# The FFN in four groups of tokens in place of three

## The chip, the cores and the metric

One core of a Trainium2 chip runs the kernel. The metric is the device time of one execution in microseconds, lower is better. Five engines matter: TensorE (PE; its weight loads are listed apart as PEld), VectorE (DVE), ScalarE (ACT), GpSimd (POOL) and SyncE (SP), which issues nearly all DMAs from one queue, in order.

## What is computed

One layer of a hybrid network, over a prompt (16 meta tokens and 2,048 frames) and a sample of 64 frames: 2,128 tokens of width 1,024. Every large product is taken in two float32r parts, as three matmuls (hi by hi, hi by lo, lo by hi).

```python
hn = rms_norm(x, norm_mix_g);  proj = hn @ w_in
o_att = diff_attention(...)      # 4 heads, causal by blocks for the prompt
o_lru = rg_lru(conv(lx)) * gelu(lg)
o_gla = gla_blocked(gq, gk, gv, log_g) * silu(gog)
x = x + concat([o_att, o_lru, o_gla]) @ w_out
hn = rms_norm(x, norm_ffn_g)
u = hn @ ffn_w_up                               # 1024 -> 2816
uc = causal_dwconv(u, ffn_conv_w, ffn_conv_b)   # 3 taps along the tokens
x = x + (gelu(uc) * (hn @ ffn_w_gate)) @ ffn_w_down
y = rms_norm(x, norm_final_g)
```

## The kernel before

The work falls into four kinds. **The projection** (`win`) multiplies six blocks of tokens by W_in. **The mixers** are two streams: `attention`, 36 units (9 chunks of tokens by 4 heads; each prompt chunk is 256 tokens and sees all keys before it), and `recurrent`, 9 chunks of RG-LRU and GLA. Their outputs go to a DRAM tensor, OT. **The FFN** takes the tokens in groups (`FGROUPS`, L67), one pass over all FFN weights per group (`ffn_group`, L1478).

A pass loads the group's rows of OT into `h2h` and `h2l` (one buffer each per block) and its residual x into `x2`. Then `wout` (L1372) multiplies by W_out, eight column tiles of 24 matmuls per block, adds to x2 (L1429) and sums the squares. `norm_ffn` turns the sums into a factor on all partitions (L383, L407, L412, L418, L393) and writes the normed rows over `h2h` and `h2l` (`normed`, L425). Then for each of 22 feature tiles `up_gate` makes two products of 24 matmuls per block (L1288), with the convolution and the gelu between, and `down` (L1337) adds finished feature tiles to x2 (L1361): two tiles at a time in all passes but the last, four in the last. After the last `down`, `final` scales x2 by its norm (L1466, L1468) and stores y. A group's x2 buffers come free only when they have been stored.

Per block, W_out has 192 matmuls, up and gate 1,056 and down 528: 1,776, whatever the block's width. With three groups the blocks are 512; 512; and 336, 256 and 512 tokens.

Each weight comes as 128x1024 parts (512 KB), one queue of parts for the whole kernel in order of use, two raw buffers and three split ones (`w_load`, `w_split`): ACT rounds the hi part, POOL (two of three) or DVE makes the lo part.

The order of the instructions is made in two steps. `Flow` merges the streams by their estimated progress: the next step comes from the stream that is least advanced for its given whole time. It decides the order of emission, which is also an instruction's priority number; the attention's numbers are lowered by 30,000 and the recurrent stream's by 16,000, the norms' by 50,000. A list scheduler then gives each engine, at each moment of its own estimate, the ready instruction with the lowest number.

```python
        for g in range(NFG - 1):
            for c, ts in enumerate(CHUNKS):
                if TILES[ts[0]][0] < FOFF[g + 1]:
                    while not (att_done[c] and rec_done[c]):
                        yield None
            yield from ffn_group(g)
    flow.run((dense(), 1875e3, 0), (attention(), 560e3, 30000), (recurrent(), 616e3, 16000))
    mstack.close()
    open3()
    flow.run((ffn_group(NFG - 1), 1.0, 0))
```

`dense` is the projection and all passes but the last. While they run, products of dense kind have three PSUM banks (`ps_w`). The last pass is emitted behind the mixers' memory: its rows, x2 and gated tiles lie where the mixers' were (`open3`), it has five more banks, and its loads are paced two at a time. With several blocks, the order of W_out's column tiles lets one block's norm be made while the other blocks' last tiles are multiplied.

Of the kernel before, what the change touches and what calls it, by code (L numbers as in the profile page):

```python
# [24 lines left out]
FFN = 2816  # L25
# [17 lines left out]
# token tiles: the sample's frames and the meta tokens, then the prompt's frames by 128  # L43
# [7 lines left out]
# the FFN's features as they are summed at a time  # L51
# [5 lines left out]
def due(g, ff):  # L57
    """the features' runs that are summed after the products of tile ff"""
    lag = 1 if g == NFG - 1 else 2
    return [q for q, r in enumerate(quads(g)[:-1]) if r[-1] + lag == ff]  # L60


# the blocks of tiles that the input projection takes, in two slots: each goes once round the projection's units, from
# the unit where it joins
WBLOCKS = [[0, 1, 2], [3, 4, 5], [6, 7, 8], [9, 10, 11], [12, 13, 14], [15, 16]]
# the groups of tokens that the FFN takes per pass over its weights, by blocks
FGROUPS = [[512], [512], [336, 256, 512]]  # L67
# the k-tiles that ACT and Pool scale at the end, by block
SHARE = [[1, 3, 5, 7], [1, 4, 7], [1, 3, 5, 7]]
NFG = len(FGROUPS)  # L70
FOFF = [sum(map(sum, FGROUPS[:g])) for g in range(NFG)]
# what the mixers take at a time: the sample with the meta tokens, then pairs of tiles
# [15 lines left out]
NPAR1 = PAR["bdm"][0]  # the rest is the mixers'  # L88
# [21 lines left out]
class Flow:  # L110
    """Order of emission: streams (generators of estimated times) merged so that they advance together."""
# [4 lines left out]
    def run(self, *streams):  # L116
        """streams: (generator, its whole time, how far it goes before the others); None from one: it waits"""
# [21 lines left out]
def tile_hymba_step(ctx, tc, xT, xkT, cache_v, wi, wo, wu, wg, wd, par, sgla, c_msk, yT_p, yT_s, nkT_p, nv_p, lh_p, lc_p, gs_p, fc_p,  # L139
# [74 lines left out]
    # ------------------------------------------------------------------ weights: one queue of parts, split ahead of use  # L214
# [58 lines left out]
    # ------------------------------------------------------------------ set-up  # L273
# [47 lines left out]
    def log1p_exp(out, tmp, z, n):  # L321
        """out = log1p(exp(-|z|)), by artanh's series in (1-t)/(3+t), t = tanh(|z|/2)."""
# [21 lines left out]
    # ------------------------------------------------------------------ norm and transposition, hi and lo  # L344
    def boost(gen, off):
        """the steps of gen, ahead of others by priority; a step after (cost, 0): in its place"""
# [12 lines left out]
    def idle(steps):  # L359
        """other products come between"""  # L360
        for _ in range(steps):
            yield 100

    def add_square(acc, k, x, small, pool=False):
        """acc += x^2, over the k-tiles"""
# [9 lines left out]
    def rsqrt_rows(acc, n, small, rb, direct=False):  # L375
        """acc: the squares of n tokens, summed up to partitions; then the tokens' norm, on all partitions"""
# [19 lines left out]
    def runs(cuts):  # L396
        """the cuts of 128 tokens together, and the shorter one"""
        full = [j for j, (_, w) in enumerate(cuts) if w == P]
        out = [(P, full[0], full[-1] + 1)] if full else []
        return out + [(w, j, j + 1) for j, (_, w) in enumerate(cuts) if w < P]  # L400
# [8 lines left out]
    def spread(r, dg, cuts, bank, tag):  # L409
        """r's rows as columns, on all partitions"""  # L410
# [10 lines left out]
    def normed(rb, gain, xs, small, H, pool=True):  # L421
        """H's hi and lo of xs by gain and norm"""
# [12 lines left out]
    def h_tiles(widths, pool, tags=("hh", "hl")):  # L435
        """hi and lo per block: [128, 8, n]"""
# [3 lines left out]
    # ------------------------------------------------------------------ W_in  # L440
    p1 = ExitStack()
    # (where the first slot and the rows lie, the outputs are loaded first after them)
# [32 lines left out]
    def first_rows(H):  # L475
        """the first block's rows go in without their norm, which is put to the products"""
# [25 lines left out]
    def columns(out, blk, ps):  # L502
        """products of the block's tokens as columns"""
# [5 lines left out]
    def rows(out, t, ps):  # L509
        """products of a tile's tokens as rows"""  # L510
        nc.scalar.activation(out=out, in_=ps, func=AF.Copy, scale=row_scale.get(t, 1.0))

    def pieces(blk):
        """(columns of the block, sample or prompt, position there)"""
# [80 lines left out]
    def win():  # L595
        H, norms = {}, {}
        for s_ in range(WSTEPS):
            u = s_ % len(UNITS)
            kind = UNITS[u][0]
            for i, blk in enumerate(WBLOCKS):  # L600
                # the block's norm is ahead of the step that it joins by as many steps as the slot is free
# [50 lines left out]
    # ------------------------------------------------------------------ the sample's cached keys  # L652
    def cached_keys():
        for h in range(4):
            ck = mp.tile([P, PAST], F32, tag="K", name="ck", bufs=2)
            if h < 2:
                # not before the first products
# [8 lines left out]
    # ------------------------------------------------------------------ mixers' outputs  # L666
    def put_ot(o, src, kt, tok0, n, scale=None):
        """scale src: [128, n] float32, tokens tok0.. of k-tile kt of the mixers' output; o: [128, 2, >= n]"""
# [8 lines left out]
    # ------------------------------------------------------------------ RG-LRU, feature-major  # L677
# [93 lines left out]
    # ------------------------------------------------------------------ GLA: blocks of 128 tokens, the decays within  # L771
    # a block by halving (every exponent is at most 0)
    def gla(c):
# [45 lines left out]
        # from and to the blocks' ends  # L819
# [30 lines left out]
        # attention within the blocks, transposed: [j, head, i]  # L850
# [40 lines left out]
        # outputs [i, (head, e)], their norm per head, and the states  # L891
# [62 lines left out]
    # ------------------------------------------------------------------ differential attention: (chunk of queries, head)  # L954
    def plan(nblk):
        """the keys' chunks of at most 512: the blocks of 128, and the meta tokens' 16 more"""
# [9 lines left out]
    class Unit:  # L966
# [26 lines left out]
        def p(self, ci, ti, m):  # L993
            """the exponentials of a chunk, a tile of queries, a map: [128, ..]"""
# [6 lines left out]
    # in halves: a map's  # L1001
    slots = {"free": 2 * NPC}

    def unit_S(u):
        """scores, chunk-wise exponentials and their statistics"""
# [618 lines left out]
```

## Time and profile before

| | us |
|---|---|
| three runs | 2980.53, 2981.39, 2983.62 (median 2981.39) |
| span of the profiled execution | 2982.7 |

The page gives no time of the profiled execution other than its span, which is 1.3 us over the median of the runs. A row of the trace gives an instruction's start, its duration, its line and what it writes from what. Matmuls overlap in the pipeline (a 512-column matmul is shown as 390 to 400 ns long), so what matmuls cost is read from their spacing: so many in so many microseconds. In a table by stretches, each engine has its busy time and, in brackets, its number of instructions; then come TensorE's granted clock (1.00 is full speed, 2.4 GHz), the DMA engines' busy share and GB/s.

### The profile page before, as it was taken

Reading aid. Unit: us, or ns where it says so; the run is one execution under the profiler, and the core shown is the slowest. Engines: PE = TensorE matmul, PEld = TensorE weight load, DVE = VectorE, ACT = ScalarE, POOL = GpSimd, SP = SyncE. Lnnn points to the kernel's source line nnn. Section 1 sums busy time; section 2 is a strip of 40 time slices with the busy share of each in tenths; the row PEclk is TensorE's granted clock in tenths of the full one; section 3 lists DMA queues with packets and bytes.
Section 4 is the critical chain, followed back from the end, with each engine's and each line's share of the span. In section 5 each row is a group of like instructions: output and inputs, shape, how many; then the busy total and the mean of one; then the engine's idle time right before and its main releaser. Section 6 shows DMA issues by size and latency. Waiting matters only on the chain. (4 is left out here: it accounts for less than half of the span.)

```text
span 2982.7 us, 44483 instructions
## 1 busy us (share of the span) xinstructions
PE 2846.8 (95%) x16031; PEld 2505.3 (84%) x16031; DVE 2087.4 (70%) x3829; ACT 1276.4 (43%) x2737; POOL 1135.1 (38%) x1310
## 2 busy tenths in 40 slices
PE   7999999999899998998998999999999999999998
PEld 7988899988777887877776787878889999989997
DVE  7677685878889899899989877545565444444445
ACT  5354554555555464564454443333242222223233
POOL 4435534434435545355335444333232222212122
PEclk9999999999999999999999999999999999999999
DMA  7675664755763444443563343463111111111111
GB/s 241 200 216 145 183 212 149 206 182 165 239 195 117 127 148 124 122 151 120 190 199 113 123 146 98 130 212 128 43 36 44 44 48 43 43 43 43 43 43 69
DMA packets 235307, 382.23 MB, mean 128 GB/s; under 512 B 26278, under 2 KB 165294, under 8 KB 235086
## 3 DMA queue, kind: packets, MB, share of 16 engines
q1 hardware_dynamic: 234942, 379.38, 40.8%
q8 instruction: 127, 2.08, 0.3%
q14 instruction: 94, 0.77, 0.1%
q10 hardware_dynamic: 144, 0.01, 0.0%
HBM read 305.15 MB, written 74.16 MB: 127 GB/s over the span
## 5 line engine op out<-in xcount | busy, mean ns | idle before, releaser
L253 POOL TENSOR_TENSOR wlo<-raw,whi 128x1024 fp32r<-128x1024 f32 (+1 forms) x202 | 491.2, 2433 | 790.1 <-ACT whi L154 725.6
L154 ACT ACTIVATE whi<-raw 128x1024 fp32r<-128x1024 f32 (+2 forms) x308 | 322.5, 1047 | 542.3 <-PE pd L1355 265.0
L1355 PE MATMUL pd<-gh,whi 128*128 128x512 f32 (+2 forms) x880 | 317.1, 364 | 23.8 <-DVE x L1361 19.1
L1052 ACT ACTIVATE pc<-ps_sc,NB 128x512 f32<-128x512 f32 (+6 forms) x400 | 224.2, 561 | 260.7 <-DVE NB L1051 213.0
L1288 PE MATMUL pu<-h2l,whi 128*128 128x512 f32 (+2 forms) x880 | 315.5, 359 | 4.6 <-DVE h2l L160 4.2
L1288 PE MATMUL pu<-h2h,whi 128*128 128x512 f32 (+2 forms) x880 | 316.3, 359 | 2.3 <-ACT h2h L154 2.2
L1288 PE MATMUL pg<-h2h,wlo 128*128 128x512 f32 (+2 forms) x880 | 314.5, 357 | 2.2 <-POOL wlo L253 1.7
L1288 PE MATMUL pg<-h2h,whi 128*128 128x512 f32 (+2 forms) x880 | 316.2, 359 | 0.3 <-DVE cc L1323 0.3
L1355 PE MATMUL pd<-gl,whi 128*128 128x512 f32 (+2 forms) x880 | 315.8, 360 | 0.3 <-DVE gl L160 0.3
L1355 PE MATMUL pd<-gh,wlo 128*128 128x512 f32 (+2 forms) x880 | 315.1, 358 | 0.0
L1288 PE MATMUL pg<-h2l,whi 128*128 128x512 f32 (+2 forms) x880 | 314.9, 358 | 0.0
L1288 PE MATMUL pu<-h2h,wlo 128*128 128x512 f32 (+2 forms) x880 | 314.7, 358 | 0.0
L1361 DVE TENSOR_TENSOR x<-x,pd 128x512 f32<-128x512 f32 (+2 forms) x320 | 193.9, 614 | 160.8 <-PE pd L1355 159.0
L1312 DVE SCALAR_TENSOR_TENSOR cc<-uh,prm,cc 128x512 f32<-128x512 f32 (+4 forms) x264 | 190.7, 729 | 162.0 <-ACT cc L1310 158.6
L631 PE MATMUL ps_w<-hh,whi 128*128 128x384 f32 (+2 forms) x768 | 259.2, 340 | 15.3 <-ACT whi L154 10.6
L1051 DVE TENSOR_REDUCE NB<-ps_sc 128x1 f32<-128x512 f32 (+6 forms) x400 | 208.7, 528 | 75.1 <-PE ps_sc L1049 74.0
L631 PE MATMUL ps_w<-hl,whi 128*128 128x384 f32 (+2 forms) x768 | 259.7, 339 | 0.5 <-DVE hl L160 0.5
L631 PE MATMUL ps_w<-hh,wlo 128*128 128x384 f32 (+2 forms) x768 | 256.4, 336 | 0.3 <-DVE wlo L160 0.3
L1355 PEld LDWEIGHTS pd<-gh,whi 128*128 128x128 f32 x880 | 166.7, 190 | 50.8 <-DVE x L1361 24.9
L157 POOL TENSOR_SCALAR pc<-pc,fr 128x512 f32<-128x512 f32 (+4 forms) x200 | 158.7, 811 | 92.3 <-DVE fr L1072 68.7
L1288 PEld LDWEIGHTS pu<-h2l,whi 128*128 128x128 f32 x880 | 165.9, 189 | 26.8 <-DVE h2l L160 5.7
L1288 PEld LDWEIGHTS pu<-h2h,whi 128*128 128x128 f32 x880 | 166.3, 189 | 24.7 <-ACT h2h L154 3.2
(330 smaller groups left out, 7090.4 us busy)
## 6 DMA issues: line engine op xcount, KB each, us to landing
raw<-in_wi SPq DMA_DIRECT2D x74, 512.0 KB
raw<-in_wu SPq DMA_DIRECT2D x66, 512.0 KB
raw<-in_wg SPq DMA_DIRECT2D x66, 512.0 KB
raw<-in_wd SPq DMA_DIRECT2D x66, 512.0 KB
Kc<-KHL SPq DMA_DIRECT2D x48, 512.0 KB
V<-VHL SPq DMA_DIRECT2D x48, 512.0 KB
Q<-QHL SPq DMA_DIRECT2D x64, 256.0 KB
raw<-in_wo SPq DMA_DIRECT2D x24, 512.0 KB
```

Source lines behind the costliest of these rows:

```text
L154: nc.scalar.activation(out=out, in_=in_, func=AF.Copy, scale=scale)
L157: nc.gpsimd.tensor_scalar(out, in_, s, 1.0, ALU.mult, ALU.mult)
L253: nc.gpsimd.tensor_tensor(out=lo[:, :n], in0=t[:, :n], in1=f(hi[:, :n]), op=ALU.subtract)
L631: nc.tensor.matmul(ps[:, :n], lhsT=wx, rhs=hx, start=st_, stop=sp_)
L1051: nc.vector.tensor_reduce(NB[:qw, ti, m, ci:ci + 1], ps[:qw, :kt_], AX.X, ALU.min)
L1052: nc.scalar.activation(out=pv_[m][:qw, :kt_], in_=ps[:qw, :kt_], func=AF.Exp, scale=-1.0, bias=NB[:qw, ti, m, ci:ci + 1], accum_out=SS[:qw ...
L1288: nc.tensor.matmul(ps[:, :n], lhsT=w_[wi_][:, k * P:(k + 1) * P], rhs=hx, start=(k == 0 and i3 == 0), stop=(k == KT - 1 and i3 == 2))
L1312: nc.vector.scalar_tensor_tensor(out=cc[:, :m], in0=uh[:, w:w + m], scalar=cw[w], in1=cc[:, :m], op0=ALU.mult, op1=ALU.add)
L1355: nc.tensor.matmul(ps[:, :n], lhsT=w_, rhs=g_[:, o:o + n], start=(j == 0 and i3 == 0), stop=(j == len(gts) - 1 and i3 == 2))
L1361: nc.vector.tensor_tensor(x2[b, ct], x2[b, ct], ps[:, :n], ALU.add)
```

## The change

The last group loses its block of 512 tokens, and this block becomes a group of its own, which `dense` takes as its third pass. The blocks' widths stay 512, 512, 512, 336, 256. The estimated whole times that `Flow` is given are 2,409 in place of 1,875 for `dense`, and 700 in place of 616 for the recurrent stream; the attention's 560 stays. The rest adapts to two blocks in the last group: what is loaded, the order of blocks in its last `down`, and which tiles ACT and POOL scale at the end (block 0: three, block 1: four; before, block 0: four, block 1: three, block 2: four). Comments went too; they are left out here.

```diff
-FGROUPS = [[512], [512], [336, 256, 512]]
-SHARE = [[1, 3, 5, 7], [1, 4, 7], [1, 3, 5, 7]]
+FGROUPS = [[512], [512], [512], [336, 256]]
+SHARE = [[1, 4, 7], [1, 3, 5, 7]]
...
         if done:
-            bs = (2, 0, 1) if nb == 3 else range(nb)
+            bs = range(nb)
...
         if len(blocks) > 1:
             load_out(1)
-            load_out(2)
             load_x2(0, [0, 1])
-            load_x2(1, [2])
         else:
             load_x2(-1, [0])
...
-                if k in SHARE[b if g == NFG - 1 else 1]:
+                if k in SHARE[b if g == NFG - 1 else 0]:
...
-    flow.run((dense(), 1875e3, 0), (attention(), 560e3, 30000),
-             (recurrent(), 616e3, 16000))
+    print("FLOW",flow.run((dense(), 2409e3, 0), (attention(), 560e3, 30000),
+             (recurrent(), 700e3, 16000)))
```

## Rows read from the trace of the kernel before

**Rows 1.** The page: the span, the engines' busy time over it, and two lines of the span in 40 slices (tenths busy).
```profile
span 2982.7 us, 44483 instructions
PE 2846.8 (95%) x16031; PEld 2505.3 (84%) x16031; DVE 2087.4 (70%) x3829; ACT 1276.4 (43%) x2737; POOL 1135.1 (38%) x1310
PE   7999999999899998998998999999999999999998
DVE  7677685878889899899989877545565444444445
```

**Rows 2.** The table by stretches: the projection; the first pass; the second pass beside mixers and after them; the last pass's step from W_out to up; the rest of it; the end. Columns: stretch and its length, then PE, PEld, DVE, ACT, POOL busy, granted clock, DMA share, GB/s.
```profile
0.00:800.00 800.00, 750.44 (x4880) 709.42 (x4880) 594.47 (x1265) 409.15 (x1006) 352.20 (x398) 0.97 0.63 192
800.00:1480.00 680.00, 641.18 (x3146) 523.51 (x3147) 606.40 (x1178) 354.73 (x820) 319.02 (x390) 0.97 0.48 148
1480.00:1925.00 445.00, 421.91 (x2091) 345.87 (x2091) 354.33 (x578) 211.31 (x436) 194.02 (x191) 0.98 0.42 131
1925.00:2048.00 123.00, 120.27 (x529) 99.53 (x528) 71.06 (x87) 39.55 (x52) 47.08 (x47) 0.99 0.57 186
...
2148.00:2176.00 28.00, 21.48 (x121) 18.11 (x121) 27.03 (x46) 13.59 (x30) 14.32 (x17) 0.96 0.09 33
2176.00:2964.00 788.00, 787.50 (x4660) 715.61 (x4659) 378.07 (x588) 218.07 (x349) 178.26 (x241) 1.00 0.13 42
2964.00:2983.00 19.00, 4.05 (x17) 2.76 (x15) 10.94 (x22) 5.34 (x11) 9.96 (x11) 0.63 0.58 210
```

**Rows 3.** Where mixers and passes stand. First the last step of an attention unit (L1182, one per unit), counted on DVE in two stretches, and its 28th and last occurrence; then a late step of a recurrent chunk (L907, four per chunk) with its first and last start; then the last `down` matmul of the second pass.
```profile
0.00:1344.00 1344.00, 12.40 (x28) 0.97 0.57 174
1344.00:1930.00 586.00, 3.77 (x8) 0.98 0.43 136
L1182 DVE SCALAR_TENSOR_TENSOR oSs<-oSs,g,ps_on x1: 461/461/461, 1342.6 to 1342.6; 128x256 f32<-128x256 f32 x1
L1182 DVE SCALAR_TENSOR_TENSOR oSs<-oSs,g,ps_on x1: 476/476/476, 1922.9 to 1922.9; 128x256 f32<-128x256 f32 x1
L907 PE MATMUL ps_r<-gvr,qkd x36: 376/379/601, 148.1 to 1725.8; 128*128 128x256 f32 x32, 64*128 64x256 f32 x4
2051.70 0.40 PE L1355 MATMUL pd<-gl,whi 128*128 128x512 f32 x1
```

**Rows 4.** Spacing of matmuls. First up and gate (L1288), then down (L1355), in 54.5 us of the second pass after the mixers; then three pieces of the chain that ended last, in the last pass: 24 matmuls of 512, of 336 and of 256 columns (start, length, count).
```profile
1971.70:2026.20 54.50, 43.68 (x192) 36.00 (x192) 1.00 0.40 126
1971.70:2026.20 54.50, 11.35 (x49) 9.07 (x49) 1.00 0.40 126
2272.30 5.60 PE pu L1288 x24
2283.50 3.72 PE pu L1288 x24
2293.75 2.83 PE pg L1288 x24
```

**Rows 5.** The step from one pass to the next, in order of time (start, duration, engine, line, what). Ahead of the first pass: the first load of rows and the first W_out matmul. From the first pass to the second: the loads of x2 and the first addition to it. From the second pass to the last: the first scaling of x2, the stores of y, the next loads of x2.
```profile
807.40 0.36 SPq L148 DMA_DIRECT2D h2h<-OT  x1
816.22 0.40 PE L1423 MATMUL pd<-h2h,whi 128*128 128x512 f32 x1
1510.86 2.00 SPq L148 DMA_DIRECT2D x<-in_xT  x3
1520.57 1.27 DVE L1429 TENSOR_TENSOR x<-x,pd 128x512 f32<-128x512 f32 x2
2064.47 0.75 DVE L1468 SCALAR_TENSOR_TENSOR x<-x,prm,ps_nb 128x512 f32<-128x512 f32 x1 [0.79 <-PE ps_nb L418]
2065.24 5.47 SPq L151 DMA_DIRECT2D out_y_prompt<-x  x7
2070.88 0.94 SPq L148 DMA_DIRECT2D x<-in_xT  x2
```

**Rows 6.** The second pass's step from W_out to up, in order of time: the last W_out matmul, the last sum of squares, the factor, the first normed rows, the first up matmul.
```profile
1562.58 0.39 PE L1423 MATMUL pd<-h2l,whi 128*128 128x512 f32 x1
1565.21 2.43 DVE L370 TENSOR_TENSOR acc<-acc,sq 128x512 f32<-128x512 f32 x1
1574.40 0.60 ACT L393 ACTIVATE acc<-ps_nb 128x512 f32<-128x512 f32 x1 [0.97 <-PE ps_nb L418]
1575.04 2.08 DVE L425 SCALAR_TENSOR_TENSOR y<-x,prm,acc 128x512 f32<-128x512 f32 x3 [0.35 <-ACT acc L393]
1576.51 0.50 PE L1288 MATMUL pu<-h2h,whi 128*128 128x512 f32 x1 [0.43 <-ACT h2h L154]
2051.16 0.68 DVE L370 TENSOR_TENSOR acc<-acc,sq 128x512 f32<-128x512 f32 x1
```

**Rows 7.** The end, in order of time: the last product, two scalings of the 512 block that are still to be done then, the factor of the last block.
```profile
2964.24 0.28 PE L1355 MATMUL pd<-gl,whi 128*128 128x256 f32 x1
2967.26 1.21 DVE L1468 SCALAR_TENSOR_TENSOR x<-x,prm,ps_nb 128x512 f32<-128x512 f32 x2
2973.47 1.22 PE L418 MATMUL ps_nb<-dg,ones 128*128 128x256 f32 x2 [3.54 <-DVE dg L412]
```

## The prediction

> **What bounds the kernel now.** I read the page first: over the whole span TensorE is busy 95%, DVE 70% [rows 1]. The slices say that this is no one kind of stretch: DVE is at 5 to 9 tenths, mostly 8 or 9, in the first 25 slices and at 4 to 6 after that, while PE stays at 8 to 9. So I cut the span into stages [rows 2]. In the projection and in the two passes that have mixers beside them, PE stands still a little: 680 - 641.2 = 38.8 us in the first pass and 445 - 421.9 = 23.1 us in the second, 61.9 us together, with DVE busy 606.4 / 680 = 89% and 354.3 / 445 = 80%. In the last pass PE is idle 0.5 us of 788, with DVE at 48%. The last pass is bound by matmuls alone; the passes with mixers lose something to a crowded DVE.
>
> That makes the idea plain: take 512 tokens from the stage with a free DVE and put them where the mixers crowd it, so that PE has more to do there. Whether it works hangs on where the mixers are when the third pass runs, so the next view is the order of events [rows 3]. The attention ends at 1922.9, the recurrent stream at 1725.8, and the second pass ends at 2051.7. So now the mixers are gone 129 us before a third pass of `dense` could begin. The rows that this pass needs (tokens up to 1,535, seven chunks, 28 units) were finished at 1342.6: it never had to wait for the mixers, but it has to wait for the second pass, whose row buffers and weights come ahead of its own.
>
> **Do the mixers stay longer?** `Flow` gets new whole times, by which `dense` is emitted 2409 / 1875 = 1.28 times as far ahead of the attention. But an attention instruction's number is lowered by 30,000, and all instructions but the weight loads are 44,483 - 16,031 = 28,452 [rows 1]: none of the projection or the passes can be numbered ahead of it, except the few boosted steps, whatever the shares are. The trace agrees. By the code's own estimates (6 x 512 x 0.425 ns per two k-tiles) a pass comes to 387 us and the projection to 483, so at the second pass's end `dense` has used some 1,260 of its 1,875, and by its share the attention would stand near two thirds. In the trace it is over by then. What holds the mixers is their own chain of small steps and DVE, not their place in the emission. I take it that they end near 1923 again, that the first 2,050 us stay as they are, and that the third pass runs alone between 2050 and 2480.
>
> **The change part by part.** The number of matmuls does not change: five blocks of 1,776 before and after, of the same widths. What changes is where the 512 block runs and what stands around it.
>
> Removed: the 512 block's part of the last pass. There 24 matmuls take 5.60 us [rows 4], so 1,776 take 414.4 us.
>
> Added: the same 1,776 in a pass of their own. After the mixers the second pass shows 192 + 49 = 241 of them in 54.5 us [rows 4], 0.2261 us each: 401.6 us. The other bound is the last pass's own spacing, 414.4. I take 401.6, since the third pass uses the second's buffers and not those of the last.
>
> Its stalls within the 22 feature tiles: after the mixers the second pass is idle 123 - 120.3 = 2.7 us of 123 [rows 2], which over 1,584 x 0.2261 = 358 us makes 8. Bounds: nothing, as in the last pass, and 23.1 / 445 of it, 19, as beside mixers.
>
> Its beginning: the rows come in time. Their load starts when the second pass's last up product has read the buffer; then two runs of `down` follow, 96 x 0.2261 = 21.7 us, and ahead of the first pass the first W_out matmul came 8.8 us after the first load [rows 5]. The x2 buffers are late instead. The second pass's x2 is normed, scaled and stored before it can be loaded over: the first scaling stands 12.8 us and the next load 19.2 us behind its last matmul [rows 3, 5]. At the step from the first pass to the second the first addition came 9.7 us after such a load [rows 5], on a crowded DVE; the other bound is at once. So the first addition is 19.2 to 28.9 us behind, and without one no PSUM bank is freed: three banks hold 3 x 24 x 0.2261 = 16.3 us of products, two only 10.9 while the other carries the factor of the final norm. The stall is between 2.9 and 18 us. I take 8, nearer to the low end, since DVE is then free. Beside mixers this is filled with their products; alone it is not.
>
> Its norm: in the second pass 13.9 us lie between the last W_out matmul and the first up matmul [rows 6], filled with the mixers' products. In a group of one block nothing of its own can fill it. The sum of squares took 2.43 us there against 0.68 when it has DVE to itself [rows 6], so the idle chain is about 12. Behind such a hole the clock falls: 0.96 and 0.63 are the means granted in the two stretches that hold idle PE [rows 2]. I add 3 for that: 15. Bounds: 9.2, the time from the last product to the last factor at the end [rows 7], and 13.9 + 5.4 = 19.3 with one product of 24 at half the clock.
>
> The last pass with two blocks: its step from W_out to up now idles 28 - 21.5 = 6.5 us [rows 2]. The first block's norm was covered by the last two tiles of both other blocks, 48 x (0.1179 + 0.2333) = 16.9 us [rows 4]; it will have 5.7. The chain of about 12 then shows 6 us ahead of the first product, and less is left behind it: +3, between 0 and +11.2, the cover lost.
>
> The end: 18.5 us lie between the last product and the span's end, and scalings of the 512 block are among them [rows 7]. They will be gone: -3, between -5 and 0.
>
> Costed at nothing: the 74 further weight parts. The stretch after the mixers splits parts at the same rate that the third pass will, with ACT at 32%, POOL at 38%, DVE at 58% and 186 GB/s, and PE idle 2% [rows 2].
>
> Sum: 401.6 + 8 + 8 + 15 - 414.4 + 3 - 3 = +18.2 us. On the profiled execution's 2982.7 this is 3000.9; the median of the runs is 1.3 lower: **3000 us**. With every term at its low end it is -5.6, with every one at its high end +67 (414.4 + 19 + 18 + 19.3 - 414.4 + 11.2); with each halfway the forecast's own range is 2986 to 3022.
>
> **The rivals.** *The third pass does run beside mixers* (faster). For it: the emission's shares are moved by 1.28, and DVE at 89% in the first pass is what a thinner mix would relieve. Against it: the numbers above. Its price: the three stops of the third pass are covered (-31), and of the 61.9 us of idle PE half to all is filled: 18.2 - 31 - 31 to -62, so 2907 to 2938. It decides when the last L1182 comes later than the end of the second pass's last `down`, 129 us later than now. The Trainium skill speaks for it (Perfetto Trace Analysis, Optimization Strategy: where the most-contended engine changes over time, interleaving the regimes may help). The same page (Identifying the Most-Contended Engine) would have TensorE judged by its weight loads' busy share and not by the matmuls'. By that, the room beside mixers is larger: 869.4 us of loads in 1,125 us, 77%, against 715.6 in 788, 91%, or 168 us and not 62.
>
> *The stops are filled from the last pass* (about no change). The mixers' memory is free from 1923, so the last pass's rows could be there early and its W_out come forward into the holes. Against it: its weights stand behind the third pass's in one queue with three buffers. Price: 18.2 - 8 - 15 = -5, so 2976.
>
> *The third pass runs like a mixed or a last pass* (slower still): spacing 0.2333 (+12.8) and stalls at 5.2% (+11), so +42 and 3023. It decides if moving the block to the second pass's buffers does not keep their spacing.
>
> **How the numbers follow.** Forecast 0.60, slower rival 0.14, faster by interleaving 0.14, filled stops 0.12. Less than 0.2%, 6 us, can't be told from no change by these runs. The forecast is slower by more than that in 0.56 and within it in 0.04; the slower rival is slower; interleaving is faster; filled stops split evenly. Slower 0.70, same 0.10, faster 0.20. The range 2974 to 3030 holds the forecast, the slower rival and most of the filled stops, and leaves out interleaving.
>
> **What would show it.** The last L1182 near 1923 and the first 2,000 us unchanged; W_out's third run of 192 starting near 2050, with DVE near 58% beside it; a stop of some 8 us in it and one of 12 to 15 behind it, with the clock below 1 there; 24 up matmuls in 5.4 us and not 5.6; the last pass some 490 us long; the end a few us shorter. A last L1182 beyond 2050 would make the forecast wrong at its root; a spacing of 0.2333 would in size only.

## The result, and the profile after

The changed kernel takes 3006.38 us in the median of four runs (2999.85 to 3006.93), against 2982.51 for the kernel before beside it: a ratio of 1.0073, with a 95% interval of 1.0058 to 1.0087. It is slower, as forecast, 6 us above the forecast's 3000 and well within its range. The profiled execution is the lowest of the four (2999.85, span 2997.8); the other three are some 6 us longer than what the rows below show.

The page, three lines as in [rows 1]:

```profile
span 2997.8 us, 44981 instructions
PE 2843.7 (95%) x16031; PEld 2509.9 (84%) x16031; DVE 2210.9 (74%) x3895; ACT 1350.0 (45%) x2810; POOL 1249.5 (42%) x1350
DVE  7676766868799899899899787656665566755566
```

TensorE's share is the same 95%. The last 14 slices of DVE are at 5 to 7, where they were at 4 to 6 in [rows 1].

The table by stretches, columns as in [rows 2]: the projection; the first pass; the second beside mixers and after them; the step into the third pass; its W_out; its norm; its feature tiles; the last pass's step from W_out to up; the rest of it; the end.

```profile
0.00:770.00 770.00, 713.06 (x4668) 677.72 (x4668) 563.55 (x1181) 382.80 (x921) 337.51 (x369) 0.98 0.62 189
...
786.00:1480.00 694.00, 652.57 (x3175) 532.42 (x3174) 618.92 (x1198) 357.25 (x830) 301.00 (x388) 0.95 0.47 144
1480.00:1990.00 510.00, 491.93 (x2439) 404.81 (x2437) 406.05 (x644) 245.58 (x501) 229.59 (x225) 0.98 0.42 131
1990.00:2058.00 68.00, 66.80 (x293) 54.34 (x291) 44.59 (x52) 24.35 (x32) 29.18 (x30) 1.00 0.79 266
2058.00:2070.00 12.00, 3.48 (x11) 2.62 (x11) 7.13 (x15) 2.73 (x4) 1.03 (x1) 0.66 0.31 87
2070.00:2115.00 45.00, 44.88 (x193) 36.53 (x191) 22.00 (x21) 13.28 (x18) 15.87 (x8) 0.98 0.52 167
2115.00:2127.00 12.00, 3.58 (x11) 1.93 (x12) 5.97 (x10) 3.24 (x5) 3.35 (x2) 0.71 0.22 75
2127.00:2491.00 364.00, 364.00 (x1608) 301.59 (x1608) 222.00 (x259) 129.54 (x168) 138.67 (x111) 1.00 0.31 94
...
2541.00:2547.00 6.00, 2.03 (x15) 1.69 (x13) 4.98 (x13) 2.32 (x4) 2.84 (x4) 0.97 0.57 162
2547.00:2982.00 435.00, 434.81 (x3172) 433.72 (x3173) 269.36 (x421) 159.77 (x271) 155.79 (x183) 0.99 0.25 75
2982.00:2998.00 16.00, 3.80 (x18) 2.48 (x16) 6.82 (x20) 3.94 (x8) 6.58 (x9) 0.66 0.45 155
```

The third pass does run alone, with two holes of 12 us in which TensorE is busy 3.5 us and the granted clock falls to 0.66 and 0.71. Its feature tiles have no idle TensorE at all. But the first 2,000 us did not stay as they were. The attention's units and the recurrent chunks by their late steps, as in [rows 3]; then, from the order of time, the second pass's last `down` matmul and the third pass's first of W_out:

```profile
L1182 DVE SCALAR_TENSOR_TENSOR oSs<-oSs,g,ps_on x36: 291/472/481, 172.4 to 1991.1; 128x256 f32<-128x256 f32 x32, 128x80 f32<-128x80 f32 x4
L907 PE MATMUL ps_r<-gvr,qkd x36: 376/378/483, 145.5 to 1685.1; 128*128 128x256 f32 x32, 64*128 64x256 f32 x4
```

```profile
2057.18 0.39 PE L1355 MATMUL pd<-gl,whi 128*128 128x512 f32 x1
...
2069.47 1.42 PE L1421 MATMUL pd<-h2h,whi 128*128 128x512 f32 x1
```

The attention ends 68 us later (1991.1 against 1922.9), the recurrent stream 41 us earlier. The projection's last product starts at 770.0 and not at 798.7, so by then 29 us had been won; the two passes lose it again and more. In [rows 3] the second pass's last `down` stands at 2051.7, with 24 matmuls of 336 columns of the last pass's W_out already mixed in from 2040.0 on (3.7 us, [rows 4]); without them it would be about 2048.0. So the second pass ends about 9 us late. From there the rest is a plain sum: 2057.2 + 12.3 (to the first W_out matmul) + 45.2 (W_out) + 11.8 (to the first up matmul) + 364.6 + 491.3 (last pass) + 15.3 (end) = 2997.7.

### The profile page after: what moved, and what is told of

It is laid out like the page before. It is cut to its first block, busy times and chain, and to the rows that moved or that the text cites. A ratio compares the mean times of both kernels' runs of the same rounds, so it can differ in the third digit from the quotient of the medians.

```text
span 2997.8 us, 44981 instructions
## 1 busy us (share of the span) xinstructions
PE 2843.7 (95%) x16031; PEld 2509.9 (84%) x16031; DVE 2210.9 (74%) x3895; ACT 1350.0 (45%) x2810; POOL 1249.5 (42%) x1350
## 4 chain that ended last, share of the span: by engine, by line
PE 64%; DVE 18%; DMA 6%; issue 5%; ACT 3%; POOL 3%; SPq 1%; POOLq 0%; ACTq 0%; DVEq 0%
PE pu L1288 15%; PE pd L1355 14%; PE pg L1288 13%; PE ps_w L631 5%; PE pd L1421 4%; PE ps_w L633 3%; DVE pc L1090 3%; PE ps_o L1156 3%; DVE BD L876 2%; PE ps_sc L1049 2%; DVE NB L1051 1%; PE ps_sc L1042 1%; PE ps_pt L1141 1%; PE ps_r L881 1%; POOL pc L157 1%
## 5 line engine op out<-in xcount | busy, mean ns | idle before, releaser
L253 POOL TENSOR_TENSOR wlo<-raw,whi 128x1024 fp32r<-128x1024 f32 (+1 forms) x251 | 608.9, 2427 | 724.6 <-ACT whi L154 681.5
L154 ACT ACTIVATE whi<-raw 128x1024 fp32r<-128x1024 f32 (+1 forms) x382 | 399.6, 1048 | 524.8 <-PE pd L1355 216.7
L1288 PE MATMUL pu<-h2h,whi 128*128 128x512 f32 (+2 forms) x880 | 317.0, 360 | 7.8 <-ACT h2h L154 3.9
L1312 DVE SCALAR_TENSOR_TENSOR cc<-uh,prm,cc 128x512 f32<-128x512 f32 (+4 forms) x264 | 213.4, 816 | 146.9 <-ACT cc L1310 142.8
L1355 PE MATMUL pd<-gh,whi 128*128 128x512 f32 (+2 forms) x880 | 313.5, 362 | 4.5 <-DVE x L1361 2.5
L1288 PE MATMUL pu<-h2l,whi 128*128 128x512 f32 (+2 forms) x880 | 316.2, 359 | 0.0
L1288 PE MATMUL pg<-h2h,whi 128*128 128x512 f32 (+2 forms) x880 | 315.6, 359 | 0.0
L1288 PE MATMUL pu<-h2h,wlo 128*128 128x512 f32 (+2 forms) x880 | 315.0, 358 | 0.0
L1288 PE MATMUL pg<-h2h,wlo 128*128 128x512 f32 (+2 forms) x880 | 314.7, 358 | 0.0
L1288 PE MATMUL pg<-h2l,whi 128*128 128x512 f32 (+2 forms) x880 | 314.2, 357 | 0.0
L1355 PE MATMUL pd<-gh,wlo 128*128 128x512 f32 (+2 forms) x880 | 313.0, 357 | 0.0
L1355 PE MATMUL pd<-gl,whi 128*128 128x512 f32 (+2 forms) x880 | 312.8, 357 | 0.0
L1361 DVE TENSOR_TENSOR x<-x,pd 128x512 f32<-128x512 f32 (+2 forms) x360 | 219.8, 622 | 95.5 <-PE pd L1355 94.1
L631 PE MATMUL ps_w<-hh,whi 128*128 128x384 f32 (+2 forms) x768 | 257.5, 337 | 19.2 <-ACT whi L154 10.7
L157 POOL TENSOR_SCALAR gh<-cc 128x512 fp32r<-128x512 f32 (+4 forms) x132 | 70.0, 533 | 343.3 <-DVE cc L1325 213.4
L160 DVE TENSOR_TENSOR wlo<-raw,whi 128x1024 fp32r<-128x1024 f32 (+2 forms) x131 | 166.2, 1268 | 53.9 <-ACT whi L154 53.6
L1288 PEld LDWEIGHTS pu<-h2h,whi 128*128 128x128 f32 x880 | 167.6, 190 | 31.4 <-ACT h2h L154 6.2
```

The costliest lines, as they stand in the source:

```text
L154: nc.scalar.activation(out=out, in_=in_, func=AF.Copy, scale=scale)
L157: nc.gpsimd.tensor_scalar(out, in_, s, 1.0, ALU.mult, ALU.mult)
L160: nc.vector.tensor_tensor(out, a, b, ALU.subtract)
L253: nc.gpsimd.tensor_tensor(out=lo[:, :n], in0=t[:, :n], in1=f(hi[:, :n]), op=ALU.subtract)
L631: nc.tensor.matmul(ps[:, :n], lhsT=wx, rhs=hx, start=st_, stop=sp_)
L1288: nc.tensor.matmul(ps[:, :n], lhsT=w_[wi_][:, k * P:(k + 1) * P], rhs=hx, start=(k == 0 and i3 == 0), stop=(k == KT - 1 and i3 == 2))
```

## The experiments

All ratios are to the kernel before, run on the same chip beside each experiment, with 95% intervals. The last L1182 is the attention's end, as above.

| label | groups | whole times | leads | attention ends | median, us | ratio |
|---|---|---|---|---|---|---|
| the change | 4 | 2409, 700 | 30000, 16000 | 1991 | 3006.4 | 1.0073 (1.0058 to 1.0087) |
| e1 | 4 | 1875, 616 | 30000, 16000 | 1924 | 2987.4 | 1.0021 (1.0010 to 1.0032) |
| e2 | 3 | 2409, 700 | 30000, 16000 | 1992 | 3001.3 | 1.0064 (1.0048 to 1.0080) |
| e3 | 4, third emitted last but one | 1875, 616 | 30000, 16000 | 1913 | 2996.3 | 1.0046 (1.0030 to 1.0062) |
| e4 | 4 | 2409, 700 | 5000, 3000 | 2250 | 2970.1 | 0.9963 (0.9950 to 0.9977) |
| e5 | 4 | 2409, 700 | 3000, 1800 | 2374 | 2976.9 | 0.9984 (0.9970 to 0.9997) |
| e6 | 3 | 1875, 616 | 4000, 2400 | 2012 | 2981.8 | 0.9996 (0.9985 to 1.0008) |
| e7 | 4 | 2409, 700 | 7000, 4000 | 2048 | 2975.4 | 0.9981 (0.9970 to 0.9992) |
| e8 | as e1, less one norm | 1875, 616 | 30000, 16000 | 1921 | 2973.4 | 0.9976 (0.9965 to 0.9988) |
| e9 | 4 | 1500, 616 | 30000, 16000 | 1852 | 3006.3 | 1.0079 (1.0062 to 1.0096) |
| e10 | 4 | 1875, 616 | 5000, 3000 | 2057 | 2989.5 | 1.0020 (1.0008 to 1.0032) |
| e11 | 4 | 1875, 616 | 3000, 1800 | 2273 | 2981.5 | 0.9994 (0.9981 to 1.0007) |
| e12 | 3 | 2409, 700 | 5000, 3000 | 2049 | 3013.6 | 1.0111 (1.0089 to 1.0132) |

### The change's two halves, one at a time (e1, e2)

The grouping alone, with the whole times of before:

```diff
-    print("FLOW",flow.run((dense(), 2409e3, 0), (attention(), 560e3, 30000),
-             (recurrent(), 700e3, 16000)))
+    flow.run((dense(), 1875e3, 0), (attention(), 560e3, 30000),
+             (recurrent(), 616e3, 16000))
```

> The four groups with Flow's old whole times (1875 and 616). Theory: the new whole times alone moved the mixers (attention's end 1923 to 1990, the projection's end 799 to 770) and cost some 6 to 9 us at the second pass's end (2048 to 2051.7 before, 2057.4 after). Then here the projection ends near 799, the last L1182 stands near 1923, the second pass's last down near 2048 to 2052, and what follows is as long as in the changed kernel (2997.9 - 2057.4 = 940.5): 2989 to 2992 us. Rival: the grouping itself moved them (less is emitted behind the mixers): last L1182 near 1990, and 2998 to 3006.

The reverse, the three groups with the new whole times (the same two numbers changed in the kernel before):

> The three groups of before with Flow's new whole times (2409 and 700). Theory: projection's end near 770, the last L1182 near 1990, and the last pass begins 6 to 9 us later: 2988 to 2991 us. Rival, the grouping moved the mixers: as before, 2981 to 2984.

The attention's units in e1:

```profile
L1182 DVE SCALAR_TENSOR_TENSOR oSs<-oSs,g,ps_on x36: 285/471/482, 175.5 to 1923.7; 128x256 f32<-128x256 f32 x32, 128x80 f32<-128x80 f32 x4
```

and in e2:

```profile
L1182 DVE SCALAR_TENSOR_TENSOR oSs<-oSs,g,ps_on x36: 291/471/483, 173.6 to 1991.9; 128x256 f32<-128x256 f32 x32, 128x80 f32<-128x80 f32 x4
```

Both go as the theory said in place: the attention's end follows the whole times, not the grouping. In size both miss their range: e1 by 1.6 us on the low side (2987.4), e2 by 10 on the high side (3001.3, which is +20 us by the medians and +11.8 in its profiled span of 2994.5; the other 8 are not in any profile). So the grouping costs 0.2% and the whole times some 0.5 to 0.6%, in either grouping.

Where the whole times cost it is seen best in e2. Its first pass holds nearly the same work as before (3,173 matmuls, 1,378 of them the mixers'; before 3,183 and 1,387) but takes 692.0 us from W_out to W_out, where before it took 678.4. What TensorE waited for longest in that pass before (who, for whom, us in all, times, longest):

```profile
PE pd L1355 <- DVE x L1361: 11.7, 8, 6.2
PE ps_o L1156 <- DVE pl L160: 5.5, 4, 2.3
```

and in e2:

```profile
PE ps_r L881 <- DVE att L885: 7.9, 2, 5.3
PE ps_pt L1141 <- DVE pl L160: 5.9, 5, 2.2
PE ps_sc L1042 <- ACT pc L1052: 4.1, 5, 1.3
```

Summed over the whole pass, TensorE's idle time ahead of mixers' products is 35.9 us in e2 and 15.7 before, and ahead of the dense products 8.8 and 20.1. So in e2 mixers' products (ps_r, ps_pt, ps_sc) more often stand at the head of TensorE's queue and wait for their own steps, and what is behind them in the queue waits too. In all TensorE idles 8 us more there; the rest of the 13.6 is wider spacing and not idle time. Why the larger whole times make the attention late is open (the two were always changed together here): in the changed kernel it is 25 to 115 us behind the kernel before from its third unit on (258 us, still in the projection), and its loads of V are late there (the first at 266.9 in place of 245.2); what delays them was not tried.

### Smaller whole times still (e9)

`dense` 1500 in place of 1875, recurrent 616, otherwise e1.

> The four groups with the large leads (30000 and 16000) and still smaller whole times (1500 for dense, 616 for the recurrent stream). 1875 gave 2987, 2409 gave 3006. If a larger whole time costs because it makes the attention late within the projection (its units are 70 us later from there on) and so crowds the passes: attention's end before 1923, the projection's end after 799, and 2970 to 2985. Rival, 1875 is near a minimum and both directions cost: 2988 to 3000.

It is the rival's case, and dearer than its range: the attention ends at 1852, but the projection's last product starts at 835.5, and the ratio is 1.0079. So an early attention is not cheap by itself; of the three settings the old one is the best.

### The stop at the beginning (e8, e3)

The changed kernel's first hole in order of time: the weight splits on POOL and a sum of squares on DVE ahead of it, the last addition of a `down` product, TensorE's two instructions in it (in brackets the idle time before each and what ended it), then the first load of the third pass's x2 and the first addition to it:

```profile
2052.30 5.22 POOL L253 TENSOR_TENSOR wlo<-raw,whi 128x1024 fp32r<-128x1024 f32 x2 [6.08 <-ACT whi L154]
...
2052.76 2.50 DVE L370 TENSOR_TENSOR acc<-acc,sq 128x512 f32<-128x512 f32 x1 [0.18 <-ACT sq L368]
...
2060.39 0.68 DVE L1361 TENSOR_TENSOR x<-x,pd 128x512 f32<-128x512 f32 x1
...
2064.26 1.86 PE L383 MATMUL ps_sq<-ones,acc 128*128 128x1 f32 x8 [6.69 <-DVE acc L370]
2068.39 2.08 PE L418 MATMUL ps_nb<-dg,ones 128*128 128x512 f32 x2 [2.27 <-DVE dg L412]
...
2075.78 0.39 SPq L148 DMA_DIRECT2D x<-in_xT  x1
...
2080.72 0.69 DVE L1427 TENSOR_TENSOR x<-x,pd 128x512 f32<-128x512 f32 x1 [5.03 <-POOL wlo L253]
```

TensorE isn't waiting for x2: W_out's first product, at 2069.47, doesn't read it and starts ahead of its first load. The two small products of the second group's final norm stand in its queue ahead of W_out, and wait for the sums of squares. All else was there: the loads of W_out's rows had been issued by 2036, two of its weights were split by 2057.5, and with the addition of 2060.39 no `down` product held a bank any more. e8 leaves that factor out:

```diff
-            yield from boost(rsqrt_rows(acc, n, env["ev"], rb, True), 0)
+            if g != 1:
+                yield from boost(rsqrt_rows(acc, n, env["ev"], rb, True), 0)
...
-                if k in SHARE[b if g == NFG - 1 else 0]:
+                if g == 1:
+                    pass
+                elif k in SHARE[b if g == NFG - 1 else 0]:
```

> The four groups with Flow's old whole times (2987 us), and the second group's y stored without its final norm: its squares are summed, but the factor (ps_sq, dg, ps_nb) and the eight scalings are left out, so that its part of y is not normed. Theory: the third pass's first stop, 12.3 us from the last down matmul to the first of W_out, is TensorE's products queued behind the factor's chain; without it W_out follows at once: 10 to 12 us less, 2975 to 2978. Rival, the stop is a bank, rows or weights that come late: it stays, 2984 to 2988.

The first load of the third pass's x2, the last `down` of the second pass and the first W_out matmul behind it, in e8:

```profile
2038.14 0.39 SPq L148 DMA_DIRECT2D x<-in_xT  x1
...
2041.50 0.39 PE L1355 MATMUL pd<-gl,whi 128*128 128x512 f32 x1
2043.10 0.47 PE L1421 MATMUL pd<-h2h,whi 128*128 128x512 f32 x1 [1.21 <-issue]
```

1.6 us in place of 12.3, and the ratio falls from 1.0021 to 0.9976, some 13 us, a little more than expected. This is a price, not a version, since that part of y is not normed. It is also the price of two things at once: without the factor the x2 buffers are stored and loaded early as well, from 2038.14 on. In the changed kernel the first load of x2 lands at 2080.5 (the bracket above names a weight split that ends 0.2 us later), the first addition to it comes 23.5 us behind the last `down` matmul (2080.72 against 2057.18), and three banks hold 16.3 us of products. So if W_out only stood ahead of the factor in the queue, an estimate from these numbers leaves some 7 us of stop, at x2; no run separates the two.

e3 gives the third pass the mixers' memory and eight banks:

```diff
-            load_x2(0, [0, 1])
+            load_x2(-1, [0])
+            load_x2(0, [1])
         else:
-            load_x2(-1, [0])
+            load_x2(0, [0])
...
-        for g in range(NFG - 1):
+        for g in range(NFG - 2):
...
+    flow.run((ffn_group(NFG - 2), 1.0, 0))
     flow.run((ffn_group(NFG - 1), 1.0, 0))
```

> The four groups, with Flow's old whole times, but the third is emitted behind the mixers like the last: its rows and x2 lie in the mixers' place, its products have eight PSUM banks, and its x2 need not wait for the second group's y. Theory: the stop of 12 us at its beginning goes (the products no longer stand behind the final norm's chain), the 12 us at its norm stay. If 512-column matmuls are spaced by where their rows lie, they come here 24 in 5.60 us as in the last pass before: 2051.7 + 0.5 + 414.4 + 12 + 491.3 + 15.3 = 2985. If it is by the kind of pass, 24 in 5.44 us: 402.6 in place of 414.4, 2973. Rival: the stop is not the shared buffers' and stays, 2985 to 2997.

Its third pass's feature tiles, the step from there into the last pass, and two runs of 24 matmuls of 512 columns in the third pass (start, length):

```profile
2095.00:2465.00 370.00, 370.00 (x1583) 297.92 (x1584) 219.74 (x256) 130.08 (x166) 139.87 (x117) 1.00 0.33 104
2465.00:2476.00 11.00, 2.64 (x13) 1.61 (x11) 3.97 (x10) 2.10 (x3) 3.90 (x7) 0.75 0.67 217
```

```profile
2113.52 5.60 PE pg L1288 x24
2119.12 5.60 PE pu L1288 x24
```

The stop in front of the third pass is gone (W_out begins at 2027.4, ahead of the last `down`), but one of 11 us now stands in front of the last pass, whose W_out in turn queues behind the third group's factor (TensorE idles 3.59 us ahead of ps_sq and 4.77 ahead of ps_nb there). And the spacing is 5.60, the slow value of [rows 4], with the same block in a pass of the same kind. So the spacing goes with where the tiles lie, not with the kind of pass. The median (2996.3, ratio 1.0046) is above both of the theory's sums and within the rival's range, though the stop did go from where the rival kept it: the moved stop was in neither sum.

### Holding the mixers back (e4, e5, e7)

In the changed kernel the leads let the attention run as far ahead as it can. Smaller leads let Flow's shares hold it back:

```diff
-(attention(), 560e3, 30000), (recurrent(), 700e3, 16000)
+(attention(), 560e3, 5000), (recurrent(), 700e3, 3000)
```

> The changed kernel, with the mixers' leads cut from 30000 and 16000 to 5000 and 3000, so that the shares of Flow hold them back and the last attention unit runs beside the third pass. Interleaving as in the forecast's first rival: the last L1182 beyond 2100, no stop at the third pass's start and at its norm (-24), and the 62 us of idle TensorE of the mixed passes filled by a third to all: 2915 to 2960. Against it, by the forecast's view that idle TensorE beside mixers is the mixers' own and goes where they go: -24 at the most, and 28 to 60 us of third pass that run at 5% idle: 2980 to 3000.

e4's first pass, second pass, third pass beside the attention and behind it:

```profile
772.00:1410.00 638.00, 610.82 (x2938) 497.12 (x2938) 537.61 (x1017) 319.50 (x729) 275.18 (x353) 0.96 0.46 143
1410.00:1971.00 561.00, 537.88 (x2544) 440.57 (x2542) 473.46 (x774) 258.81 (x483) 253.76 (x241) 0.98 0.43 134
1971.00:2250.00 279.00, 273.08 (x1370) 225.96 (x1369) 206.15 (x314) 131.19 (x262) 122.82 (x113) 0.99 0.41 132
2250.00:2461.00 211.00, 210.81 (x937) 174.79 (x936) 127.79 (x150) 73.25 (x94) 80.61 (x72) 1.00 0.41 132
```

and its attention's units:

```profile
L1182 DVE SCALAR_TENSOR_TENSOR oSs<-oSs,g,ps_on x36: 290/470/482, 174.6 to 2249.9; 128x256 f32<-128x256 f32 x32, 128x80 f32<-128x80 f32 x4
```

This is the interleaving that the forecast's first rival meant, and it is the fastest kernel of the study: 2970.1 us, 0.37% under the kernel before and 1.1% under the change, between the two ranges expected. Idle TensorE from the first pass's W_out to the last pass falls from 77.7 us in the changed kernel (41.4 + 18.1 + 1.2 + 8.5 + 0.1 + 8.4) to 56.4 (27.2 + 23.1 + 5.9 + 0.2). Two things make most of that up: in the first pass, with DVE at 84% in place of 89%, TensorE idles 14 us less, and the third pass has mixers' products where it had two holes. Not all of the gain lies there: of the 28.7 us between the two profiled executions 13.6 are had before the first pass's W_out begins (772.1 against 785.7), where only some 4 us of the mixers' own matmul time have been moved away. The forecast put its price at -62 to -93 us against its own sum; by the ratios e4 is 33 us under the change.

e7 (leads 7000 and 4000) spreads the first two passes but leaves the third alone; e5 (3000 and 1800) pushes further.

> The changed kernel with leads of 7000 and 4000: the attention ends where the second pass ends, so that the first two passes are spread as with a small lead and the third still runs alone after its first stop. If covering the third pass is the gain: last L1182 near 2060, 2985 to 3000. If the spreading over the first two passes is: 2970 to 2980.

> The changed kernel with leads of 3000 and 1800, so that the attention ends still later in the third pass than with 5000 and 3000 (2250 us, 2970 us in all). Theory: work of the mixers taken out of the crowded first two passes and put beside the third, which had stood alone, is the gain; more of it in the third pass gains more: last L1182 near 2350, 2955 to 2968 us. Rival: what was gained was the cover of the third pass's two stops, which is had already: 2967 to 2975.

e7's first pass and the third pass's two holes:

```profile
788.00:1429.00 641.00, 617.47 (x3060) 506.17 (x3060) 557.25 (x1064) 335.41 (x778) 288.71 (x365) 0.98 0.48 150
...
2029.00:2041.00 12.00, 8.71 (x43) 6.54 (x41) 8.91 (x20) 4.75 (x10) 4.99 (x7) 0.76 0.19 57
...
2088.00:2100.00 12.00, 3.43 (x12) 1.75 (x12) 5.89 (x10) 3.09 (x5) 3.54 (x3) 0.72 0.57 199
```

In e7 the third pass stands alone with its holes (the first part filled), and still 0.91% of the 1.1% is won, as its second case expected: most of the gain is how the mixers are spread over the first two passes (1,252.1 us from the first W_out to the third, against 1,283.8 in the change). e5 missed the theory, and its rival by 2 us: more work beside the third pass is not better. Why, a sum over all matmuls shows: take each at the spacing that three in ten of its kind stay below over these runs, call the rest of the stretch lost, and set it against the mixers' own matmul time there (worked out from the traces, us; told apart more or less finely, the kinds shift the first pass's two columns by some 10 us against each other):

```
                 first pass        third pass
                 mixers  lost      mixers  lost
before           174     101       -       -
the change       172     119       1       14
e1               174     102       1       14
e7               158      79       2       15
e4               143      91       61      23
e11              122      70       51      28
e5                99      63       103     56
```

Over the mixed passes of these kernels a line fits: 0.65 us lost for each us of mixers' products (0.5 to 0.76 by how the kinds are told apart), less some 10 (correlation 0.92 to 0.94; the holes in front of a third pass left out). So the loss goes where the mixers go, and moving them doesn't win the 62 us that the forecast's rival wanted to fill. What is won lies in the scatter about the line, which these runs don't explain: the change's first pass is some 16 us above it, e7's some 15 below.

### Are the four groups needed? (e6, e10, e11, e12)

e10 and e11 are e4 and e5 with the old whole times; e6 and e12 are three groups with small leads, e12 with all of e4's numbers.

> The four groups with Flow's old whole times (1875, 616) and leads of 5000 and 3000: the attention is spread and ends about where the second pass ends. If what the small lead repairs is only the lateness that the new whole times brought, there is little left for it to repair here: 2983 to 2989, as with the old whole times and the large leads (2987). If spreading the mixers over the passes is a gain of its own: 2965 to 2976.

> The four groups with the old whole times and leads of 3000 and 1800: the attention ends a third into the third pass, as with 2409 and 5000 (2970 us), but is not late in the projection. If the two gains add: 2955 to 2966. If the place of the attention's end and the spread alone count: 2966 to 2975.

> The three groups of before, with leads of 4000 and 2400 in place of 30000 and 16000: the attention is held back within the two passes that there are. Theory, the fourth group is needed for the gain, since the lead only spreads the mixers over the passes that dense has: 2975 to 2985. Rival, the small lead alone is the gain, whatever the groups are: 2960 to 2970.

> The three groups of before with the whole times and the leads of the fastest kernel so far (2409 and 700; 5000 and 3000; 2970 us with four groups): the attention is spread over the two passes that there are and ends with the second. If the fourth group is needed for the gain, since with it the mixers go beside a third pass too: 2980 to 2992. If the leads alone make the gain: 2966 to 2974, and the fourth group buys nothing.

With the old whole times the small leads bring nothing (e10: 1.0020, as e1, half a us above its first range) or 0.3% against e1 (e11, above both of its ranges). With three groups they bring nothing (e6) or cost 1.1% (e12), more than either side expected. Why, e12 shows in its attention's units:

```profile
L1182 DVE SCALAR_TENSOR_TENSOR oSs<-oSs,g,ps_on x36: 291/473/482, 176.4 to 2049.2; 128x256 f32<-128x256 f32 x32, 128x80 f32<-128x80 f32 x4
```

the first product of the last pass, with its wait:

```profile
2060.11 0.62 PE L1423 MATMUL pd<-h2h,whi 128*128 128x336 f32 x1 [2.46 <-DMA h2h<-OT]
```

and the stretch of that pass's W_out:

```profile
2061.00:2181.00 120.00, 101.97 (x590) 92.31 (x589) 37.00 (x58) 20.87 (x36) 21.07 (x30) 0.93 0.48 149
```

Its second pass ends at 2046.4 (before, without the mixed-in matmuls, 2048.0), but the last pass's rows and x2 lie in the mixers' memory, which now comes free only then: its W_out starts 14 us behind the second pass and idles 18 of 120 us. With the same order numbers the four groups are 1.5% faster (0.9963 against 1.0111). The third pass is what gives late mixers room. With the leads that the change keeps, no mixers are left to use it.

## Why the prediction was right, and where not

**The sign and the time** came out, the size by luck: two errors cancel. The grouping was put at +18 and measured +6 (e1), the whole times were put at nothing and measured some +16 (the change against e1 by the ratios; 10.4 between their profiled executions). The forecast's halfway range is 2988 to 3024 by its own terms and not 2986 to 3022, which changes nothing here.

**"The first 2,050 us stay as they are"** failed. The step was the reading that a lead of 30,000 makes the shares irrelevant. With the lead no dense step is numbered ahead of the attention, that is so; but the order of emission acts on the attention in the projection all the same (e2: its end 69 us later with nothing but the shares changed). What was right is the conclusion for the third pass: 1991 is still ahead of 2057, and the pass runs alone.

**Spacing**: right. 24 matmuls in 5.44 us, as this view of the third pass shows (start, length), against 5.60 in [rows 4]; the last pass's blocks kept theirs:

```profile
2144.86 5.44 PE pg L1288 x24
2150.30 5.44 PE pu L1288 x24
2581.10 3.71 PE pg L1288 x24
2584.81 2.83 PE pu L1288 x24
```

With `down` at 0.2314 in the last pass before, the block's matmuls cost 10.7 us less (forecast 12.8).

**Stalls in the feature tiles**: put at 8, measured 2.0: 364.8 us in e1, less 1,584 x 0.2267 = 359.1 and 3.7 of the last pass's W_out that is mixed in. The row taken, the second pass after 1925, has no rate to be read from it: its 2.7 us are a single wait, at 1969.08, of a `down` product for the additions to x2. These stood in DVE's queue behind the split of a weight whose load landed late (ACT waits for it until 1966.12), among the last pass's loads of rows.

**The beginning**: put at 8, measured 12.1, by another mechanism. The x2 buffers are as late as forecast (in the changed kernel the first load 18.6 us and the first addition 23.5 us behind the last `down` matmul, put at 19.2 and at 19.2 to 28.9), but they are not what W_out waits for; it queues behind the final norm's factor, and the wait for x2 passes under that. The forecast priced the bank that the factor takes and not its place in TensorE's queue.

**The norm**: put at 15, measured 11.8, of which the chain of waits shows 4.16 us behind the last sum of squares, 2.25 behind the factor and 2.14 behind the first normed rows:

```profile
2119.04 1.05 PE L383 MATMUL ps_sq<-ones,acc 128*128 128x1 f32 x8 [4.16 <-DVE acc L370]
2122.34 2.07 PE L418 MATMUL ps_nb<-dg,ones 128*128 128x512 f32 x2 [2.25 <-DVE dg L412]
2126.55 0.80 PE L1288 MATMUL pu<-h2h,whi 128*128 128x512 f32 x1 [2.14 <-ACT h2h L154]
```

The 12 of the chain came out, though not as reckoned: they left out the slow sum of squares, as a matter of a crowded DVE, and it is in the 11.8 again (2.41 us, last section). The 3 for the clock show in part behind the first hole instead, where W_out takes 45.5 us in e1 for 192 matmuls, 2.0 above 192 x 0.2267.

**The last pass's step**: put at +3, measured the other way. Beside its matmuls the last pass takes some 8 us less in e1 than before. Spacings above the usual at the step sum to 9.0 us in e1 and 12.8 before; in the last `down` runs, where before a third block's norm came in, 0.9 and 4.0; 1 us is not placed. The forecast counted the cover that is lost and not that one block fewer has a norm to be covered.

**The end**: -3, measured 15.4 against 18.5. Sum for e1: -1.7 (its second pass ends at 2046.2, before at 2048.0 without the mixed-in matmuls) - 10.7 + 2.0 + 2.0 + 12.1 + 11.8 - 7.7 - 3.1 = +4.7, its span against that of before (the 7.7 of the last pass is what is left over by this sum).

**Interleaving** was given 0.14 and its test, a last L1182 behind the second pass's end, was not met by the change. Once it is met (e4), the rival's sign is right and its price a third to a half of what was written: 33 us, against 62 to 93. The Trainium skill (Perfetto Trace Analysis, Optimization Strategy) says that interleaving such stretches may improve the time; e4, 33 us under the change, agrees. e12 goes the other way, 1.1% above the kernel before, since its last pass gets its memory late. The larger room that the prediction read from the weight loads, 77% against 91% or 168 us, sets unlike matmuls side by side. In the changed kernel's table two stretches have next to no idle TensorE: in the third pass's feature tiles, 512 columns wide, the weight loads are busy 301.59 of 364 us, 83%; in the last pass's, 336 and 256 wide, 433.72 of 435. So that share goes with the width of the matmuls, and the 91% of a pass with narrow blocks is no measure for blocks of 512.

## What to carry over

A pass that is cut out of a merged stage pays at its two serial steps, here 12 us each, unless something independent is queued there; whether the other stream will still be there is set by the order's parameters, so try these with the regrouping and not after it. Price idle time beside a second stream as that stream's (here 0.5 to 0.76 us lost per us of its products): most of it moves along when the stream is moved. And look in the in-order queue for what stands ahead of the first product of a stage, before asking which buffer it lacks.

## What was not expected of the hardware

Matmuls of 512 columns are spaced 0.2267 us with rows and tiles in the second pass's buffers, and 0.2333 (0.2314 in `down`) in the mixers' place; e3 has the same block, widths and weights there and shows the slow value, so it is the place, 10.7 us in a block's 1,776 matmuls. What in the place does it was not tried; blocks of 336 and 256 columns show 3.71 and 2.83 us per 24 there.

A sum of squares on DVE (L370) takes 0.68 us where no weight split on POOL (L253) runs. In the changed kernel 11 of those over 512 columns start while a split runs; they take 1.70 to 2.52 us, and each ends 0.54 to 0.56 us behind that split's end. The last one ahead of the third pass's norm:

```profile
2116.10 2.34 POOL L253 TENSOR_TENSOR wlo<-raw,whi 128x1024 fp32r<-128x1024 f32 x1 [3.04 <-ACT whi L154]
...
2116.57 2.41 DVE L370 TENSOR_TENSOR acc<-acc,sq 128x512 f32<-128x512 f32 x1 [0.97 <-ACT sq L368]
```

The Trainium skill (SBUF — State Buffer, SBUF: two separate sides) has a DVE instruction with two SBUF inputs and a GpSimd instruction that reads SBUF share a pair of ports, which the one that starts first locks for its whole length; these rows agree. So 1.7 us of the third pass's hole at its norm are a weight split's, and two more such sums (2.50 and 2.29 us) stand ahead of the hole at its beginning.
